# Twelve dense quads in layer 1's down projection, ten in layer 2's, and five-row products in the last norm

## The chip, the cores and the metric

The kernel runs on one core of a Trainium2 chip. The metric is the device time of one execution in microseconds; the median of three runs is compared. The core's engines work side by side and meet at semaphores: TensorE (PE; its weight loads are listed as PEld), VectorE (DVE), ScalarE (ACT), GpSimd (POOL) and SyncE (SP). In this kernel SP issues nearly all transfers, GpSimd a few.

## The reference

Two decoder layers over 256 tokens of width 2048, in float32. Layer 1 attends within one causal block (its list of past blocks is empty at this length), layer 2 in a sliding window of 128 with sinks. Each layer ends in a gated feed-forward with a causal convolution, and every sublayer is followed by a residual and a layer norm:

```
for layer in range(2):
    attn = moba(h) if layer == 0 else swa(h)
    h = layer_norm(ALPHA * h + attn, ln_g[layer, 0], ln_b[layer, 0])
    g, v = split(conv(h @ w_up) + conv_b)            # w_up: 2048 x 11008
    ffn  = (gelu(g) * v) @ w_down                    # w_down: 5504 x 2048
    h = layer_norm(ALPHA * h + ffn, ln_g[layer, 1], ln_b[layer, 1])
# layer_norm(x) = (x - mean) * rsqrt(var + eps) * g + b
```

## The kernel before

**Blocks and halves.** All matrix products run in the rounded format fp32r, three times each: every operand is split into a high and a low part, and high x high, high x low and low x high are added in PSUM. Weights come from DRAM in *halves*, tiles of 128 x 1024 numbers (0.5 MB), each of two *blocks* of 128 x 512. For each half SP loads `raw`, ScalarE rounds the high part `wh` (line 164), and VectorE subtracts to get the low part `wl` (line 173). Seven `raw` buffers and four pairs of `wh` and `wl` are in rotation, so a half is split when the half four before it has been used up. In a projection a block product is three matmuls of 512 columns: lines 389 to 391, or 618 to 620 where quads are used.

**Slots.** One step of the program order is one half. `take()` hands out the next half after it has emitted the split of the half three ahead; `at(n, f)` puts a small piece of work n halves later into the order. Every engine executes its own part of this order strictly in sequence.

**Quads.** In the down projection (43 k-blocks, four column chunks of 512, two token halves) a *quad* is 2 k-blocks x 2 column chunks x 2 token halves. A scheme of Strassen's kind makes it in 7 block products instead of 8. It needs sums of weight blocks, which are added up beforehand in DRAM (`sum_weights`: two copies on SP, three accumulating transfers on GpSimd, lines 301 to 309; `plan_sums` spreads them over earlier stages), and sums of activations (`pair_sums` and `four_sums`; for k-blocks 0 to 15 during the up projection, for later ones, the *late sums*, at the start of the down projection on VectorE and ScalarE). `QUADS[l][n]` is the number of quads of layer l for chunk pair n (0: chunks 0 and 1; 1: chunks 2 and 3; 2: the attention's output projection). `quad_halves` lays out the order: a few plain halves, then for each quad two halves of weight sums (`"t"`) and halves with single weight blocks, filled up with plain blocks, then the plain rest. The fourth single block of a quad shares a half with a plain block, or, where `DENSE` is true, with the fourth block of the next quad. In `two_chunks` the partial results `a`, `s1`, `s2`, `s3` are combined afterwards (`chain`) and added to the residual in `res`.

**Where late sums and scales live.** Two tiles `gb0` and `gb1` hold the norm's scale and shift, each loaded in four pieces (`load_gb_piece`). Before that they hold the early sums, and `gb1` also holds the late sums.

**The last norm.** The last eight halves of the last layer are multiplied token half by token half (`tilewise`, `late`), so that the first token half is normalised while the second is still being multiplied. For the second, `finish` computes, for three of the four chunks, `res * g * rs + (-mean * rs) * g + b`: the product `res * g` is made ahead (`scaled`), ScalarE scales it by `rs`, and TensorE makes the rest as a product of a 2-row matrix (`-mean * rs` and ones, transposed) with two rows `g` and `b` (line 692, in float32). VectorE adds the two and SP stores. The fourth chunk takes the plain way through `norm`.

Of the kernel before, what the change touches and what calls it, by code (L numbers as in the profile page):

```python
# [11 lines left out]
F32 = mybir.dt.float32  # L12
F32R = mybir.dt.float32r
# [39 lines left out]

QUADS = ((10, 8, 4), (10, 8, 4))
DENSE = ((False, True), (False, False))
LEAD = (4, 2)
# [3 lines left out]
S_EARLY = 8  # L60
QUAD_ORDER = ((0, 1, 2, 3, 4, 5, 8, 9, 6, 7), (0, 1, 2, 3, 4, 5, 6, 7))
QUAD_LIST = [(l, n, p) for l in range(2) for n in range(3) for p in range(QUADS[l][n])]
# [3 lines left out]
def quad_halves(l, n):  # L66

    if n == 2:  # L70
        return wo_halves(l)
    q = QUADS[l][n]
    plain = [(k, c) for c in range(2) for k in range(2 * q, FT)]
    two = lambda *b: ("w", *b, *(plain.pop(0) for _ in range(2 - len(b))))
    order = [two() for _ in range(LEAD[n])]
    fourth = []
    for p in QUAD_ORDER[n][:q]:
# [29 lines left out]
def trunk(ctx: ExitStack, tc: tile.TileContext, wst, wq, xT_in, x_in, relb, onehot, umask, sinks, conv_in, ln_g, ln_b, out):  # L107
# [363 lines left out]
    def project_out(src, nk, li, homes, preload, turnover=None, paired=None, early_sums=None, wo_sums=None):  # L471
# [45 lines left out]
        if not after:  # L517
            mr = stat.tile([P, 2], F32, name="mr", bufs=1)

# [25 lines left out]
        def quad_sums(p):  # L545
# [3 lines left out]
            if p < S_EARLY:  # L549
                return xT[:, 2 * p, :], xT[:, 2 * p + 1, :]  # L550
            o = (p - S_EARLY) * 1024
            return late_sums[:, o:o + 512], late_sums[:, o + 512:o + 1024]

        def two_chunks(n, which, scratch, at_half={}):
# [55 lines left out]
            for hx, ps in enumerate(steps):  # L610
# [12 lines left out]
                if ready and hx == max(first_end, quads_end):  # L623
# [3 lines left out]
                    for t in range(2):  # L627
                        at(4, measure, n, t)
                if not ready and hx == quads_end:
# [16 lines left out]
        def norm(t, c):  # L646
# [4 lines left out]
            if not after:  # L651
                nc.sync.dma_start(out[t * P:(t + 1) * P, cs], z)

        def rows():

            for i, a in enumerate((ln_g, ln_b)):
                nc.gpsimd.dma_start(paired[i:i + 1], bass.AP(tensor=a.tensor, offset=a.offset + li * D,
                                                             ap=[[D, 1], [1, (NCH - 1) * 512]]))
            nc.vector.memset(mr, 1.0)

# [4 lines left out]
        def last_piece(i):  # L665
# [7 lines left out]
            nc.vector.bn_stats(stats[:, 1, NCH - 1 + i, :], z[:, i * 256:(i + 1) * 256])  # L673

        def finish():


            nc.vector.tensor_scalar(mr[:, 0:1], ag[1][:, 0:1], rs[1], -1.0, op0=ALU.mult, op1=ALU.mult)
            mrT = wpool.tile([P, HW], F32, name="raw")[0:2, 0:P]
# [4 lines left out]
            nc.tensor.transpose(pt[0:2, 0:P], mr, ident)  # L684
            part = lambda n: res[:, 1, n * 512:(n + 1) * 512]
            by_rs = lambda n: nc.scalar.activation(part(n), part(n), AF.Copy, scale=rs[1])
            by_rs(0)
            nc.scalar.activation(mrT, pt[0:2, 0:P], AF.Copy)
            shift = []
            for n in range(NCH - 1):  # L690
                shift.append(psum.tile([P, 512], F32, name="at"))
                nc.tensor.matmul(shift[n], mrT, paired[0:2, n * 512:(n + 1) * 512], start=True, stop=True)
            norm(1, COLS[1][-1])
            for n in range(NCH - 1):
# [22 lines left out]
        def late(t, i):  # L717
            last = i == WINDOW - 1
            if t == 0 and last:
                evac(NCH - 1, 0, accs[0])  # L720
# [15 lines left out]
            if t == 1 and last:  # L736
                if after:
                    evac(NCH - 1, 1, accs[1])
                else:
                    last_piece(1)  # L740
                sd = moments(1)
                nc.vector.reciprocal(rs[1], sd)
                if not after:
                    finish()

        if paired is not None:
            late_sums = gbp.tile([P, D], F32R, name="gb1")
            gb = scale_shift()
            last_late = max(i for i, h in enumerate(quad_halves(l, 0)) if h[0] == "w" and h[1][0] // 2 in
                            range(S_EARLY, QUADS[l][0]))  # L750
# [108 lines left out]
    def layer_attention(l, rest, stage, turnover):  # L859
# [120 lines left out]
    class FeedForward:  # L980
# [26 lines left out]
        def run(self, rest):  # L1007
# [213 lines left out]
```

## Time and profile before

| What | us |
|---|---|
| Median of three runs (lowest to highest) | 2057.65 (2057.54 to 2058.45) |
| The profiled execution's own time | 2057.03 |
| Its span, first to last instruction | 2055.3 |
| Mean granted TensorE clock | 0.999 |
| First matmul with weights starts | 5.25 |
| Layer 1's down projection: quad stages, last window | 868 to 1068, to 1115 |
| Layer 2's down projection: quad stages, last window | 1823 to 2023, to 2045 |
| Last block product starts | 2044.65 |
| Last addition ends | 2051.41 |

A row of the timeline or of the chain reads: start in us, length in us, engine, line, operation, tile written and tiles read, shape, count; in brackets the engine's idle time ahead of it and what ended it. A row of waits reads: total us, number, longest. Instructions of a group that follow each other directly are merged into one row. A row of windows gives the stretch, its length, then busy us and instructions of each engine, the granted clock, the DMA engines' busy share and GB/s.

### The profile page before, as it was taken

How to read it: one execution, taken by the hardware profiler on the slowest of the kernel's cores; microseconds unless marked ns; L12 is line 12 of the kernel's file. 1: busy time of each engine (PE TensorE's matmuls, PEld its weight loads, DVE VectorE, ACT ScalarE, POOL GpSimd, SP SyncE). 2: the span in 40 equal slices, each digit the busy share in tenths (PEclk: the TensorE clock that was granted, in tenths of full speed). 3: DMA queues.
4: the chain of work that ended last, by engine and by line, in shares of the span. 5: the costliest groups of instructions: out<-in, count | busy, mean ns of one | idle time of the engine just before them, and what ended most of it. 6: DMA issues, size and time to landing. Idle time of an engine off the chain costs nothing.

```text
span 2055.3 us, 29510 instructions
## 1 busy us (share of the span) xinstructions
PE 2048.0 (100%) x10975; PEld 1770.4 (86%) x10975; DVE 1588.5 (77%) x2384; ACT 1073.4 (52%) x1494; POOL 131.4 (6%) x152
## 2 busy tenths in 40 slices
PE   9999999999999999999999999999999999999998
PEld 7888888988888888888888888898888888888887
DVE  5665558898887878787786787988887787887767
ACT  5554446345555455565563566545455554556553
POOL 0000000001111111000000100001111110000000
PEclk9999999999999999999999999999999999999999
DMA  9888768489999999689894967839999997568883
GB/s 321 252 267 268 225 193 302 178 248 301 286 296 308 280 306 240 211 280 311 294 333 130 259 191 222 328 123 296 291 283 292 287 289 238 189 211 314 286 298 125
DMA packets 166673, 532.04 MB, mean 259 GB/s; under 512 B 19152, under 2 KB 24080, under 8 KB 166272
## 3 DMA queue, kind: packets, MB, share of 16 engines
q1 hardware_dynamic: 138656, 479.11, 65.8%
q0 software_dynamic: 27584, 50.78, 16.1%
q8 instruction: 86, 1.41, 0.3%
q14 instruction: 59, 0.48, 0.1%
q10 hardware_dynamic: 288, 0.26, 0.0%
HBM read 527.91 MB, written 98.62 MB: 305 GB/s over the span
## 4 chain that ended last, share of the span: by engine, by line
PE 100%; DVE 0%; ACT 0%; issue 0%; POOL 0%; DVEq 0%; POOLq 0%
PE acc L336 39%; PE acc L339 20%; PE acc L620 6%; PE acc L618 6%; PE acc L619 6%; PE acc L389 4%; PE acc L391 4%; PE acc L390 4%; PE at L620 2%; PE at L619 2%; PE at L618 2%; PE acc L354 1%; PE acc L366 1%; PE at L809 1%; PE at L842 1%; PE at L707 1%
## 5 line engine op out<-in xcount | busy, mean ns | idle before, releaser
L173 DVE TENSOR_TENSOR wl<-raw,wh 128x1024 fp32r<-128x1024 f32 (+1 forms) x729 | 886.2, 1218 | 397.6 <-ACT wh L164 380.6
L164 ACT ACTIVATE wh<-raw 128x1024 fp32r<-128x1024 f32 (+1 forms) x729 | 769.3, 1056 | 709.3 <-issue 243.5
L336 PE MATMUL acc<-xT,wh 128*128 128x512 f32 x3456 | 872.7, 394 | 0.0
L336 PEld LDWEIGHTS acc<-xT,wh 128*128 128x128 f32 x3456 | 623.5, 189 | 113.0
L339 PEld LDWEIGHTS acc<-xT,wl 128*128 128x128 f32 x3456 | 471.5, 190 | 33.8
L339 PE MATMUL acc<-xT,wl 128*128 128x256 f32 x3456 | 481.9, 282 | 0.0
L618 PE MATMUL acc<-wh,up 128*128 128x512 f32 x328 | 127.6, 389 | 0.0
L619 PE MATMUL acc<-wl,up 128*128 128x512 f32 x328 | 127.6, 389 | 0.0
L620 PE MATMUL acc<-wh,up 128*128 128x512 f32 x328 | 127.6, 389 | 0.0
L1031 DVE SCALAR_TENSOR_TENSOR work<-work,cw 128x255 f32<-128x255 f32 x172 | 83.2, 484 | 6.1
L1032 DVE SCALAR_TENSOR_TENSOR work<-work,cw 128x254 f32<-128x254 f32 x172 | 83.1, 483 | 6.2
L305 POOL DMA_DIRECT2D t<-in_wq_dram x44 | 54.1, 1230 | 433.2 <-DMA t<-in_wq_dram 433.0
L1030 DVE TENSOR_SCALAR work<-work,cw 128x256 f32<-128x256 f32 x172 | 71.9, 418 | 6.2
L1029 DVE TENSOR_TENSOR work<-acc,work 128x256 f32<-128x256 f32 x172 | 71.7, 417 | 1.5 <-ACT work L1028 1.5
L620 PEld LDWEIGHTS acc<-wh,up 128*128 128x128 f32 x328 | 61.6, 188 | 12.7
L618 PEld LDWEIGHTS acc<-wh,up 128*128 128x128 f32 x328 | 61.6, 188 | 12.7
L619 PEld LDWEIGHTS acc<-wl,up 128*128 128x128 f32 x328 | 61.6, 188 | 12.7
L307 POOL DMA_DIRECT2D t<-t x44 | 36.5, 829 | 480.6 <-DMA t<-in_wq_dram 468.2
L1028 ACT ACTIVATE work<-acc 128x256 f32<-128x256 f32 x172 | 63.3, 368 | 6.5 <-PE acc L366 6.5
L201 ACT ACTIVATE work<-work 128x256 f32<-128x256 f32 x86 | 36.1, 419 | 48.1 <-DVE work L1032 48.1
L389 PE MATMUL acc<-wh,xT 128*128 128x512 f32 x144 | 57.9, 402 | 0.0
L391 PE MATMUL acc<-wh,xT 128*128 128x512 f32 x144 | 56.2, 390 | 0.0
(255 smaller groups left out, 2205.1 us busy)
## 6 DMA issues: line engine op xcount, KB each, us to landing
raw<-in_wst_dram SPq DMA_DIRECT2D x699, 512.0 KB, 5.5
t<-in_wq_dram SPq DMA_DIRECT2D x88, 512.0 KB, 7.3
raw<-t SPq DMA_DIRECT2D x88, 512.0 KB, 4.5
t<-in_wq_dram POOLq DMA_DIRECT2D x44, 512.0 KB, 11.6
t<-t POOLq DMA_DIRECT2D x88, 256.0 KB, 7.1
gb<-in_ln_g_dram SPq DMA_DIRECT2D x16, 256.0 KB, 6.5
gb<-in_ln_b_dram SPq DMA_DIRECT2D x16, 256.0 KB, 8.1
band<-ud SPq DMA_DIRECT2D x4, 512.0 KB
```

Source lines behind the costliest of these rows:

```text
L164: nc.scalar.activation(wh[:, c], raws[s][:, c], AF.Copy)
L173: nc.vector.tensor_tensor(out=wl[:, c], in0=raws[s][:, c], in1=wh[:, c].bitcast(F32), op=ALU.subtract)
L336: nc.tensor.matmul(acc, cols(wh, j), xT[:, k, :], start=(k == 0), stop=False)
L339: nc.tensor.matmul(o, cols(wl, j), xT[:, k, 0:T], start=False, stop=(k == KB - 1))
L389: nc.tensor.matmul(acc, sh, wh, start=(k == first), stop=False)
L390: nc.tensor.matmul(acc, sh, wl, start=False, stop=False)
L391: nc.tensor.matmul(acc, sl, wh, start=False, stop=(k == self.nk - 1))
L618: nc.tensor.matmul(bank(key), a[0], wh[:, c], start=key not in begun, stop=False)
L619: nc.tensor.matmul(bank(key), a[0], wl[:, c], start=False, stop=False)
L620: nc.tensor.matmul(bank(key), a[1], wh[:, c], start=False, stop=stop)
L1031: nc.vector.scalar_tensor_tensor(c[:, 1:T], h[:, 0:T - 1], w[:, 1:2], c[:, 1:T], op0=ALU.mult, op1=ALU.add)
L1032: nc.vector.scalar_tensor_tensor(c[:, 2:T], h[:, 0:T - 2], w[:, 0:1], c[:, 2:T], op0=ALU.mult, op1=ALU.add)
```

## The change

Layer 1's chunks 0 and 1 get twelve quads instead of ten, in the dense layout; layer 2's chunks 2 and 3 get ten instead of eight, dense as well, and take quads 8 and 9 first. Layer 1 then has four late sums, two of them in `gb0`, so that the scale's pieces are loaded later. The preparation of weight sums is spread anew over the stages. In the last norm the products have five rows instead of two and run in fp32r: `-g` in a high, a low and again a high part, `b` in a high and a low part, against the high and low part of `mean * rs` and ones. The rows are prepared ahead in `row_parts`, stored in DRAM and read back as rows. The fourth chunk's subtraction and scaling is cut in two 256-wide pieces, one of them ahead of the reciprocal (`centre`). The measuring of chunk 2's statistics in the last layer moves into the last eight halves.

```
-QUADS = ((10, 8, 4), (10, 8, 4))
-DENSE = ((False, True), (False, False))
+QUADS = ((12, 8, 4), (10, 10, 4))
+DENSE = ((True, True), (False, True))
...
-QUAD_ORDER = ((0, 1, 2, 3, 4, 5, 8, 9, 6, 7), (0, 1, 2, 3, 4, 5, 6, 7))
+QUAD_ORDER = ((0, 1, 2, 3, 4, 5, 8, 9, 10, 11, 6, 7), (8, 9, 0, 1, 2, 3, 4, 5, 6, 7))
+SUMS_AHEAD = (3, 2)
...
-            mr = stat.tile([P, 2], F32, name="mr", bufs=1)
+            mr = stat.tile([P, 5], F32R, name="mr", bufs=1)
+            parts = stat.tile([P, 5, 12], F32R, name="parts", bufs=1)
+            as_rows = dram.tile([5, (NCH - 1) * 512], F32, name="rows")
+            rank = []
...
-            o = (p - S_EARLY) * 1024
-            return late_sums[:, o:o + 512], late_sums[:, o + 512:o + 1024]
+            s, o = late_sums[(p - S_EARLY) // 2], p % 2 * 1024
+            return s[:, o:o + 512], s[:, o + 512:o + 1024]
...
-                        at(4, measure, n, t)
+                        if after or not n:
+                            at(4, measure, n, t)
...
+        def row_parts():
+            sg = stat.tile([P, 2, 12], F32, name="sg", bufs=1)
+            for i, a in enumerate((ln_g, ln_b)):
+                nc.gpsimd.dma_start(sg[:, i, :], bass.AP(tensor=a.tensor, offset=a.offset + li * D,
+                                                         ap=[[12, P], [1, 12]]))
+            nc.vector.tensor_scalar(sg[:, 0, :], sg[:, 0, :], -1.0, None, op0=ALU.mult)
+            for i in (0, 2):
+                nc.scalar.activation(parts[:, i, :], sg[:, 0, :], AF.Copy)
+            nc.scalar.activation(parts[:, 3, :], sg[:, 1, :], AF.Copy)
+            minus(parts[:, 1, :], sg[:, 0, :], parts[:, 0, :].bitcast(F32))
+            minus(parts[:, 4, :], sg[:, 1, :], parts[:, 3, :].bitcast(F32))
+            nc.gpsimd.dma_start(as_rows.rearrange("r (p c) -> p r c", c=12), parts.bitcast(F32))
+            nc.vector.memset(mr.bitcast(F32), 1.0)
+
         def rows():
...
-            nc.vector.memset(mr, 1.0)
+            nc.gpsimd.dma_start(paired[0:5, 0:(NCH - 1) * 512], as_rows)
+            for c, w in ((0, 1024), (1024, 512)):
+                rank.append(wpool.tile([P, HW], F32R, name="raw")[0:5, 0:w])
+                nc.scalar.activation(rank[-1], paired[0:5, c:c + w], AF.Copy)
...
+        def centre(half):
+            z = slice(D - 512 + half * 256, D - 256 + half * 256)
+            nc.vector.scalar_tensor_tensor(res[:, 1, z], res[:, 1, z], ag[1][:, 0:1], gb[0][:, z],
+                                           op0=ALU.subtract, op1=ALU.mult)
...
-            nc.vector.tensor_scalar(mr[:, 0:1], ag[1][:, 0:1], rs[1], -1.0, op0=ALU.mult, op1=ALU.mult)
+            mean = ag[1][:, 0:1]
+            nc.vector.tensor_scalar(mr[:, 0:1], mean, rs[1], None, op0=ALU.mult)
+            nc.vector.tensor_scalar(mr[:, 1:2], mean, rs[1], None, op0=ALU.mult)
+            nc.vector.scalar_tensor_tensor(mr[:, 2:3], mean, rs[1], mr[:, 0:1].bitcast(F32), op0=ALU.mult,
+                                           op1=ALU.subtract)
...
-                nc.tensor.matmul(shift[n], mrT, paired[0:2, n * 512:(n + 1) * 512], start=True, stop=True)
-            norm(1, COLS[1][-1])
+                nc.tensor.matmul(shift[n], mrT, rank[n // 2][:, n % 2 * 512:n % 2 * 512 + 512], start=True, stop=True)
+            centre(1)
+            z = slice(D - 512, D)
+            nc.vector.scalar_tensor_tensor(res[:, 1, z], res[:, 1, z], rs[1], gb[1][:, z], op0=ALU.mult, op1=ALU.add)
+            nc.sync.dma_start(out[P:2 * P, z], res[:, 1, z])
...
+            if t == 0 and not after and i == WINDOW // 2:
+                for s in range(2):
+                    measure(NCH - 2, s)
...
+                if not after:
+                    centre(0)
                 nc.vector.reciprocal(rs[1], sd)
...
-            late_sums = gbp.tile([P, D], F32R, name="gb1")
+            late_sums = [gbp.tile([P, D], F32R, name=f"gb{1 - i}") for i in range((QUADS[l][0] - S_EARLY) // 2)]
...
+            if len(late_sums) > 1:
+                first, late_gaps = last_of(S_EARLY + 2) + 5, (7, 11, 13, 15)
+            else:
+                first, late_gaps = 10, (8, 15, 22, 29)
             for n in range(NCH):
-                at(10 + 8 * n, load_gb_piece, n, 0)
-                at(last_late + (7, 11, 13, 15)[n], load_gb_piece, n, 1)
+                at(first + 8 * n, load_gb_piece, n, 0)
+                at(last_late + late_gaps[n], load_gb_piece, n, 1)
...
+            if not after:
+                at(40, row_parts)
...
-        plan_sums(WO_QUADS[l][2 * l:] + [(l, 0, p) for p in range(2)], (18, 2)[l], (12, 10)[l])
+        plan_sums(WO_QUADS[l] + [(l, 0, p) for p in range(SUMS_AHEAD[l])], (18, 2)[l], (11, 7)[l])
...
-            mine = [q for q in QUAD_LIST if q[0] == l and q[1] < 2][2:]
+            mine = [q for q in QUAD_LIST if q[0] == l and q[1] < 2][SUMS_AHEAD[l]:]
...
-                mine += WO_QUADS[1][:2]
...
-            plan_sums(mine, 12, (4 * FT - 30) / (len(mine) + 3))
+            plan_sums(mine, 0, (4 * FT - 18) / (len(mine) + 3))
```

More of the change, by code (lines that the diff above doesn't have):

```diff
@@ L76, in quad_halves @@
     fourth = []
-    for p in QUAD_ORDER[n][:q]:
+    for p in (p for p in QUAD_ORDER[n] if p < q):
         order += [("t", p, 0), two((2 * p, 0)), ("t", p, 1), two((2 * p + 1, 0))]
@@ L673, in last_piece @@
             nc.vector.bn_stats(stats[:, 1, NCH - 1 + i, :], z[:, i * 256:(i + 1) * 256])
+        def centre(half):
+            z = slice(D - 512 + half * 256, D - 256 + half * 256)
+            nc.vector.scalar_tensor_tensor(res[:, 1, z], res[:, 1, z], ag[1][:, 0:1], gb[0][:, z],
+                                           op0=ALU.subtract, op1=ALU.mult)
         def finish():
-            nc.vector.tensor_scalar(mr[:, 0:1], ag[1][:, 0:1], rs[1], -1.0, op0=ALU.mult, op1=ALU.mult)
-            mrT = wpool.tile([P, HW], F32, name="raw")[0:2, 0:P]
+            mean = ag[1][:, 0:1]
[3 more added lines that the diff above has]
+                                           op1=ALU.subtract)
+            mrT = wpool.tile([P, HW], F32R, name="raw")[0:5, 0:P]
             still = acc_tile()
@@ L683, in finish @@
             pt = psum.tile([P, 512], F32, name="at")
-            nc.tensor.transpose(pt[0:2, 0:P], mr, ident)
+            nc.tensor.transpose(pt[0:5, 0:P], mr.bitcast(F32), ident)
             part = lambda n: res[:, 1, n * 512:(n + 1) * 512]
@@ L687, in finish @@
             by_rs(0)
-            nc.scalar.activation(mrT, pt[0:2, 0:P], AF.Copy)
+            nc.scalar.activation(mrT, pt[0:5, 0:P], AF.Copy)
             shift = []
@@ L746, in project_out @@
         if paired is not None:
-            late_sums = gbp.tile([P, D], F32R, name="gb1")
+            late_sums = [gbp.tile([P, D], F32R, name=f"gb{1 - i}") for i in range((QUADS[l][0] - S_EARLY) // 2)]
             gb = scale_shift()
-            last_late = max(i for i, h in enumerate(quad_halves(l, 0)) if h[0] == "w" and h[1][0] // 2 in
-                            range(S_EARLY, QUADS[l][0]))
+            both = quad_halves(l, 0) + quad_halves(l, 1)
+            last_of = lambda p0: max(i for i, h in enumerate(both) if h[0] == "w" and
+                                     any(p0 <= k // 2 < QUADS[l][i >= len(quad_halves(l, 0))] for k, _ in h[1:]))
+            last_late = last_of(S_EARLY)
+            if len(late_sums) > 1:
+                first, late_gaps = last_of(S_EARLY + 2) + 5, (7, 11, 13, 15)
+            else:
+                first, late_gaps = 10, (8, 15, 22, 29)
             for n in range(NCH):
-                at(10 + 8 * n, load_gb_piece, n, 0)
-                at(last_late + (7, 11, 13, 15)[n], load_gb_piece, n, 1)
+                at(first + 8 * n, load_gb_piece, n, 0)
+                at(last_late + late_gaps[n], load_gb_piece, n, 1)
             for i, p in enumerate(range(0, S_EARLY, 2)):
```

3 lines of the change are left out of this document (removed).

## The prediction

> **What bounds the kernel now.** First the page, then who TensorE waits for:
>
> ```profile
> PE 2048.0 (100%) x10975; PEld 1770.4 (86%) x10975; DVE 1588.5 (77%) x2384; ACT 1073.4 (52%) x1494; POOL 131.4 (6%) x152
> ...
> PE at L264 <- POOL ident masks.py:199: 1.4, 1, 1.4
> PE at L684 <- DVE mr L678: 0.8, 1, 0.8
> PE at L692 <- ACT raw L688: 0.4, 1, 0.4
> ```
>
> The three waits lie before the first weight block and behind the last one. In between TensorE never waits, though a busy PE alone would not prove that, since its ends are modelled. So I went to the timeline for the distance between starts. These two rows are the first products of two blocks, thirteen blocks apart, each block three 512-wide products (L389, L390, L391):
>
> ```profile
> 2024.90 0.39 PE L389 MATMUL acc<-xT,up 128*128 128x512 f32 x1
> 2033.74 0.39 PE L389 MATMUL acc<-xT,up 128*128 128x512 f32 x1
> ```
>
> 8.84 us over 13 blocks is 0.680 us a block, 0.227 us a matmul. The 0.39 us is the length of one, not its price. What removes a block product removes 0.68 us, as long as weights arrive, and the tail behind the last product counts in full. Those are the two places where this change can earn; everywhere else it can only lose.
>
> **Block products.** A plain pair of k-blocks costs 8 block products for 2 token halves and 2 column chunks, a quad costs 7. Counting through the order of halves (`quad_halves`): layer 1, chunks 0 and 1, had 10 quads, 162 products in 58 halves; with 12 it has 160 in 61. Layer 2, chunks 2 and 3, had 8 quads, 164 products in 55 halves; with 10 it has 162 in 58. The other two stages keep theirs. Four products fewer: 4 x 0.680 = 2.72 us. This term rests on the start distance alone.
>
> The Trainium skill, "TensorE: Matmul & The Clock Gate", section "Back-to-back issue gap", gives about 131 ns per 512-wide matmul for a stream of load-and-multiply pairs; by that figure the term would be an estimated 12 x 0.131 = 1.6 us. Here the stream runs at 227 ns, so the measurement decides.
>
> **Do the weights keep up?** "Dense" packs two fourth blocks of two quads into one half, so fewer plain blocks lie between. In layer 1, chunks 0 and 1, the quad stretch goes from 130 products in 50 halves to 132 in 54: from 1.77 to 1.66 us of TensorE a half. A half is 0.524 MB, so it asks for 315 GB/s. Layer 1's second stage is already dense (88 products in 36 halves, the same 1.66 us). The three stretches are: the quad start of stage one, the middle of dense stage two, its end:
>
> ```profile
> 868.00:924.00 56.00, 56.00 (x250) 46.44 (x249) 46.23 (x53) 36.10 (x38) 0.00 (x0) 1.00 0.81 273
> 1005.00:1040.00 35.00, 35.00 (x156) 29.01 (x155) 25.62 (x21) 22.08 (x21) 0.00 (x0) 1.00 0.90 316
> 1040.00:1068.00 28.00, 28.00 (x126) 23.18 (x125) 27.68 (x30) 20.93 (x23) 0.00 (x0) 1.00 0.94 334
> ...
> ACT wh L164 <- PE acc L620: 35.8, 42, 1.7
> ```
>
> The columns after the engines' busy times are the clock, the DMA share and GB/s. Dense stage two moves 316 GB/s at a DMA share of 0.90, and 334 in the next stretch, with TensorE undisturbed. The last row (waits between 868 and 979 us) says that ScalarE's splits wait for TensorE to free a buffer, not for a load. So three more halves a stage cost nothing, covered by DMA room and by prefetch.
>
> A page's rule speaks against such density: the Trainium skill, "DMA: Bandwidth & Descriptors", section "Specifications", puts a core's share of HBM at about 358 GB/s. An estimate of 315 against 358 leaves 12% of room, so the rule, too, would allow the dense stream; the 334 GB/s measured here leaves 6%.
>
> VectorE is closer. Two more late sums (p = 10, 11) join layer 1's start, now four in a row, one every four halves. One late sum as the trace has it, with the splits between its pieces, and one split's lead:
>
> ```profile
> 892.74 1.23 DVE L173 TENSOR_TENSOR wl<-raw,wh 128x1024 fp32r<-128x1024 f32 x1 [0.46 <-ACT wh L164]
> 893.88 0.75 DVE L457 TENSOR_TENSOR work<-up 128x256 f32<-128x256 f32 x2
> 894.55 1.22 DVE L173 TENSOR_TENSOR wl<-raw,wh 128x1024 fp32r<-128x1024 f32 x1
> 895.69 0.81 DVE L440 TENSOR_TENSOR work<-work 128x128 f32<-128x128 f32 x3
> 896.42 0.28 DVE L449 TENSOR_TENSOR work<-work 128x128 f32<-128x128 f32 x1
> 896.62 1.22 DVE L173 TENSOR_TENSOR wl<-raw,wh 128x1024 fp32r<-128x1024 f32 x1
> 897.76 0.68 DVE L440 TENSOR_TENSOR gb<-work,gb 128x512 fp32r<-128x512 f32 x1
> 898.36 2.41 DVE L173 TENSOR_TENSOR wl<-raw,wh 128x1024 fp32r<-128x1024 f32 x2
> ...
> 900.49 1.06 ACT L164 ACTIVATE wh<-raw 128x1024 fp32r<-128x1024 f32 x1 [0.97 <-PE acc L620]
> 901.58 2.54 DVE L173 TENSOR_TENSOR wl<-raw,wh 128x1024 fp32r<-128x1024 f32 x2 [0.81 <-ACT wh L164]
> ```
>
> A sum takes 0.67 + 0.93 + 0.60 = 2.20 us from start to start, a split 1.14. Over the sixteen halves of four sums VectorE has 16 x 1.14 + 4 x 2.20 = 27.0 us of work, and one idle moment like the 0.46 us per two sums or so makes about 28; TensorE takes 16 x 1.66 = 26.6. The margin it eats: a split starts when the half four before it is used up, ends 1.09 + 1.22 = 2.31 us later, and is needed three halves (7 or 8 products, 4.8 to 5.4 us) after; about 2.2 us with the release. So some 1.5 of 2.2 us go, 0.5 to 1 is left: no stall, but the tightest place of the change. If the cover is gone it costs what is missing, at most the two new sums, 4.4 us. Behind it the margin refills by 1.66 - 1.14 us a half.
>
> **Sums in DRAM.** The quads' weight sums run on GpSimd's queue one after another, some 20.6 us each:
>
> ```profile
> 452.93 1.37 POOL L305 DMA_DIRECT2D t<-in_wq_dram  x1
> 473.51 1.35 POOL L305 DMA_DIRECT2D t<-in_wq_dram  x1
> ...
> 1719.12 0.81 POOL L309 DMA_DIRECT2D t<-t  x1 [6.43 <-DMA t<-t]
> 1115.00:1250.00 135.00, 135.00 (x794) 119.78 (x794) 101.05 (x230) 74.26 (x160) 12.43 (x14) 1.00 0.80 232
> ```
>
> Layer 2's attention goes from four to six of them (one every 7 halves), its feed-forward from 16 to 18, layer 1's from 18 to 17. Six need 124 us in a stretch of 135 at a DMA share of 0.80; the output projection's own four come first, from about 1140 us, and are done near 1225, before that projection begins at 1250. Layer 2's 18 need 371 us; they begin at half 0 instead of 12 (some 30 us earlier) and have two more to do (41 us), so they end some 11 us after the 1719 above; the projection that uses them begins at 1823 and loads its first about ten halves ahead. SP's loads would queue behind a sum that is late; none is. Zero. Moving layer 1's scale and shift pieces to halves 53 to 77 puts 0.26 MB transfers on SP where 4-product halves relax it; zero too.
>
> **The row parts.** At half 40 of layer 2's second stage four small VectorE and three small ScalarE instructions enter, and three transfers on GpSimd. Bounded by the 2x128 copy below (0.27 us), ScalarE's three are 0.8 us, and before them it waits one VectorE split, 1.2 us; the next split is 1.7 us late against a margin of 2.2. Zero, at worst 0.7. Their source transfer has nothing to wait for on GpSimd after 1719, so it lands long before. The two copies to the 5-row operand (at most 1.06 + 0.7 us) and the moved measurements (2 x 0.69) fall into idle time of 10.24 and 5.29 us, the first and second bracket here:
>
> ```profile
> 2046.22 0.29 ACT L640 ACTIVATE sd<-ag,eps 128x1 f32<-128x1 f32 x1 [10.24 <-DVE ag L638]
> 2033.94 0.69 DVE L514 TENSOR_TENSOR res<-acc,res 128x512 f32<-128x512 f32 x1 [5.29 <-PE acc L391]
> ```
>
> **The tail.** In order of time, and the width that `centre` uses:
>
> ```profile
> 2045.89 0.29 DVE L638 BATCH_NORM_AGGREGATE ag<-stats 128x2 f32<-128x30 f32 x1
> 2046.55 0.16 DVE L742 RECIPROCAL rs<-sd 128x1 f32<-128x1 f32 x1 [0.36 <-ACT sd L640]
> 2046.75 0.21 DVE L678 TENSOR_SCALAR mr<-ag,rs 128x1 f32<-128x1 f32 x1
> 2046.88 0.74 DVE L649 SCALAR_TENSOR_TENSOR res<-res,ag,gb 128x512 f32<-128x512 f32 x1
> 2047.01 0.27 PE L684 MATMUL at<-ident,mr 128*2 128x128 f32 x1 [0.77 <-DVE mr L678]
> 2047.38 0.27 ACT L688 ACTIVATE raw<-at 2x128 f32<-2x128 f32 x1
> 2047.56 1.32 ACT L686 ACTIVATE res<-res,rs 128x512 f32<-128x512 f32 x2
> 2047.65 0.75 DVE L650 SCALAR_TENSOR_TENSOR res<-res,rs,gb 128x512 f32<-128x512 f32 x1
> 2047.70 2.84 PE L692 MATMUL at<-work,raw 2*128 2x512 f32 x6 [0.42 <-ACT raw L688]
> 2048.86 0.69 DVE L514 TENSOR_TENSOR res<-at,res 128x512 f32<-128x512 f32 x1 [0.45 <-PE at L692]
> 2049.79 0.69 DVE L514 TENSOR_TENSOR res<-at,res 128x512 f32<-128x512 f32 x1 [0.24 <-PE at L692]
> 2050.65 0.76 DVE L514 TENSOR_TENSOR res<-at,res 128x256 f32<-128x256 f32 x2 [0.17 <-PE at L692]
> ...
> L1031 DVE SCALAR_TENSOR_TENSOR work<-work,cw 128x255 f32<-128x255 f32 x172 | 83.2, 484 | 6.1
> ```
>
> Now the three shift products pace VectorE: waits of 0.45, 0.24 and 0.17 us. In fp32r a 512-wide product starts every 0.227 us, if five rows go as fast as 128 do, instead of 0.95 us (2.84 / 3). Step by step: `centre(0)`, 0.48 us, fills the 0.36 us wait for the square root, so the reciprocal is 0.06 late. Three small instructions instead of one at 0.13 us (2046.75 to 2046.88) add 0.26: transpose at 2047.32, copy 2047.69, products 2048.01, the first ready at about 2048.5. VectorE meanwhile: `centre(1)` 2047.20, the second half of the norm 2047.71, first addition 2048.55, then 0.62, 0.62 and 0.34 on: end at 2050.55 instead of 2051.41. ScalarE's scalings move by 0.3 and stay ahead. The last output is issued and lands as long after the last addition as before, since five issues still find SP free. I take 0.8 us. From above: all waits and one 256-wide pass gone, 0.86 + 0.5 - 0.3 = 1.1. From below: five-row products no faster than those of two rows leave the 0.31 us delay, a loss of 0.3.
>
> **Sum.** 2.72 + 0.8 = 3.5 us, bounds 2.4 and 3.8. The profiled execution took 2057.03 us (span 2055.3), 0.6 below the median of 2057.65; its profile after should read about 2053.5, and the median 2057.65 - 3.5 = 2054.1, 0.17% faster. A difference of 0.2%, 4.1 us, is about what a measurement of this kernel can tell from no change, and the forecast falls just short of it.
>
> **Rivals.** *More than forecast* (0.14): even the upper bound, 3.8 us, lacks 0.3 us to 4.1; the three runs before spread over 0.9, so a median near 2053.3 can come out. *The late sums stall TensorE* (0.14): the 0.5 to 1 us of margin rests on durations read off one sum. Without it, 1 to 4.4 us come back: 2055.2 to 2058.5, mostly 2056. For it speaks VectorE at 46.23 of 56 us in that stretch before the change; against it, no wait there today. *Slower* (0.06): VectorE, in order, reaches the row parts and their source transfer has not landed; every weight split queues behind it, and TensorE behind those. The slowest kind of GpSimd's transfers:
>
> ```profile
> t<-in_wq_dram POOLq DMA_DIRECT2D x44, 512.0 KB, 11.6
> ```
>
> The last column is the median from issue to landing. If the row parts' source were issued only where it is used and took as long, 11.6 - 2.2 = 9.4 us would be lost: 2063.5. It decides once the landing is over 2.2 us late and cancels the gain at 5.7. Against it: GpSimd is free from about 1730 us, and that transfer is far smaller. That the change does not drop the four products would show as 10,975 minus less than twelve matmuls; I count it within the stall's chance, as its time is the same.
>
> **Numbers.** Forecast 0.66, with its own range of 2053.4 to 2055.2. The range 2053.2 to 2056.6 leaves out half of the first rival's lower part, the worst stalls and the slow rival, under 2 in 10. Faster 0.14, within 0.2% 0.80, slower 0.06.
>
> **What would show it.** TensorE's last product 2.7 us earlier; no new TensorE wait between 20 us and the tail, and VectorE busy over 90% around 880 to 910 us; three products in the tail within 0.9 us, and no idle of VectorE in front of the last additions; a wait of VectorE near 1999 us below 0.5 us. The forecast is wrong if the starts of the products near 905 us are more than 0.68 us a block apart, or if the tail is not shorter.

## The result and the profile after

| | before | after |
|---|---|---|
| Median us (17 runs each) | 2057.86 (2057.33 to 2058.70) | 2054.07 (2053.47 to 2054.37) |
| Profiled execution us, span | 2057.03, 2055.3 | 2054.26, 2052.5 |

The ratio is 0.9981, with a 95% interval of 0.9975 to 0.9988: 3.8 us less, where 3.5 was forecast. By the bound of 0.2% this is no difference; by its interval it is a small gain.

The page after, its engines' row, and what TensorE waited for:

```profile
PE 2043.9 (100%) x10960; PEld 1767.8 (86%) x10960; DVE 1600.8 (78%) x2410; ACT 1081.4 (53%) x1507; POOL 143.7 (7%) x166
...
PE at L265 <- POOL ident masks.py:199: 1.4, 1, 1.4
PE at L714 <- DVE mr L707: 1.1, 1, 1.1
PE at L722 <- ACT raw L718: 0.4, 1, 0.4
```

Fifteen matmuls fewer: four products of three, and three in the tail, where six float32 instructions became three. No new wait stands between the start and the tail. Where the time went shows in the timeline of TensorE, as the first product of each quad stage and the first product behind it. After:

```profile
868.86 0.40 PE L622 MATMUL acc<-wh,up 128*128 128x512 f32 x1
1067.45 0.39 PE L390 MATMUL acc<-xT,up 128*128 128x512 f32 x1
...
1822.19 0.40 PE L622 MATMUL acc<-wh,up 128*128 128x512 f32 x1
2020.77 0.39 PE L390 MATMUL acc<-xT,up 128*128 128x512 f32 x1
```

and before:

```profile
868.25 0.40 PE L618 MATMUL acc<-wh,up 128*128 128x512 f32 x1
1068.20 0.39 PE L389 MATMUL acc<-xT,up 128*128 128x512 f32 x1
...
1822.91 0.40 PE L618 MATMUL acc<-wh,up 128*128 128x512 f32 x1
2022.86 0.39 PE L389 MATMUL acc<-xT,up 128*128 128x512 f32 x1
```

Layer 1's two stages took 199.95 us and take 198.59, layer 2's 199.95 and 198.58: 1.36 and 1.37 us, two products of 0.680 each. (The profiled execution after reaches its first quad stage at 868.86, 0.6 us later than the one before, so its last block product starts only 2.08 us sooner. This differs between executions: the ten other profiles with the same first stage reach it between 868.02 and 868.80.)

The tight place, VectorE's four late sums. The windows are before and after from 880 to 910 us (busy us per engine, clock, DMA share, GB/s), each of its own kernel:

```profile
880.00:910.00 30.00, 30.00 (x134) 24.82 (x134) 25.78 (x33) 20.08 (x21) 0.00 (x0) 1.00 0.88 293
```

```profile
880.00:910.00 30.00, 30.00 (x134) 24.86 (x133) 29.27 (x45) 21.30 (x22) 0.00 (x0) 1.00 0.84 278
```

The timeline after has, behind that stretch, four splits and the first two products of the half that the first of them serves:

```profile
912.03 4.95 DVE L174 TENSOR_TENSOR wl<-raw,wh 128x1024 fp32r<-128x1024 f32 x4
914.45 0.39 PE L622 MATMUL acc<-wh,st 128*128 128x512 f32 x1
914.67 0.39 PE L623 MATMUL acc<-wl,st 128*128 128x512 f32 x1
```

VectorE went from 86 to 98% busy, and the split that ends at 913.25 (912.03 and one split of 1.22) leads the first product of its half by 1.20 us, and the second, which is the one that reads `wl`, by 1.42. That is the smallest lead of the four sums. Counted in the same way before, to the first product, no lead was under 1.9.

The row parts, on GpSimd, VectorE and ScalarE:

```profile
1727.74 0.88 POOL L665 DMA_DIRECT2D sg<-in_ln_g_dram  x1
...
2003.49 0.17 DVE L667 TENSOR_SCALAR sg<-sg 128x12 f32<-128x12 f32 x1
2003.69 0.31 ACT L669 ACTIVATE parts<-sg 128x12 fp32r<-128x12 f32 x2 [1.38 <-DVE sg L667]
2005.15 3.50 DVE L174 TENSOR_TENSOR wl<-raw,wh 128x1024 fp32r<-128x1024 f32 x3 [0.83 <-ACT wh L165]
```

GpSimd fetched their source 276 us ahead of its use. ScalarE waited 1.38 us for VectorE's split, as reckoned. The smallest lead of a split behind it is 1.47 us; before, the smallest there was 2.24.

The tail, in order of time:

```profile
2044.13 0.48 DVE L698 SCALAR_TENSOR_TENSOR res<-res,ag,gb 128x256 f32<-128x256 f32 x1
2044.54 0.15 DVE L780 RECIPROCAL rs<-sd 128x1 f32<-128x1 f32 x1
2044.98 0.22 DVE L707 SCALAR_TENSOR_TENSOR mr<-ag,rs,mr 128x1 fp32r<-128x1 f32 x1
2045.25 0.27 PE L714 MATMUL at<-ident,mr 128*5 128x128 f32 x1 [1.09 <-DVE mr L707]
2045.62 0.27 ACT L718 ACTIVATE raw<-at 5x128 fp32r<-5x128 f32 x1 [0.17 <-PE at L714]
2045.63 0.75 DVE L725 SCALAR_TENSOR_TENSOR res<-res,rs,gb 128x512 f32<-128x512 f32 x1
2045.94 0.96 PE L722 MATMUL at<-raw 5*128 5x512 f32 x3 [0.42 <-ACT raw L718]
2046.47 1.95 DVE L515 TENSOR_TENSOR res<-at,res 128x512 f32<-128x512 f32 x4
2047.19 1.94 SPq L733 DMA_DIRECT2D out_dram<-res  x4
```

Three products in 0.96 us instead of 2.84, and the four additions in one row without an idle moment. From the start of the last block product (of its last matmul, to be exact: 2042.57; before 2044.65) to the end of the last addition it is 5.86 us instead of 6.75. So far the forecast holds to 0.1 us. But the last output packet ends 8.44 us after that product instead of 8.63, and the last store lands, that is, signals its completion, 9.02 us after it instead of 9.35: of the 0.9 us only 0.2 to 0.3 is left. The DMA rows show where the rest stayed (windows of 1 us; the last two columns are the DMA engines' busy share and GB/s). After:

```profile
2046.40:2047.40 1.00, 0.50 (x3) 0.06 (x1) 0.93 (x2) 0.71 (x2) 0.00 (x0) 1.00 0.14 55
2047.40:2048.40 1.00, 0.00 (x0) 0.00 (x0) 1.00 (x3) 0.00 (x0) 0.00 (x0) 0.86 0.93 346
2048.40:2049.40 1.00, 0.00 (x0) 0.00 (x0) 0.02 (x1) 0.00 (x0) 0.00 (x0) 0.50 1.04 339
2049.40:2050.40 1.00, 0.00 (x0) 0.00 (x0) 0.00 (x0) 0.00 (x0) 0.00 (x0) 0.50 0.94 285
```

and before:

```profile
2049.40:2050.40 1.00, 1.00 (x3) 0.18 (x1) 0.76 (x2) 0.00 (x0) 0.00 (x0) 1.00 0.56 217
2050.40:2051.40 1.00, 0.14 (x1) 0.00 (x0) 0.83 (x3) 0.00 (x0) 0.00 (x0) 0.56 0.71 279
2051.40:2052.40 1.00, 0.00 (x0) 0.00 (x0) 0.00 (x1) 0.00 (x0) 0.00 (x0) 0.50 0.99 357
2052.40:2053.40 1.00, 0.00 (x0) 0.00 (x0) 0.00 (x0) 0.00 (x0) 0.00 (x0) 0.50 0.53 151
```

Before, the stores came far enough apart to leave the DMA engines gaps. After, they are full for three microseconds, two of them behind the last addition.

One more step follows the landing. SyncE closes the program with a row of waits, one for each transfer's semaphore, in a fixed order and some 0.06 us apart. What it waited for there, before and after:

```profile
SPq L1216 <- DMA out_dram<-res: 1.8, 1, 1.8
```

```profile
SPq L1261 <- DMA out_dram<-res: 1.8, 3, 0.9
```

Before, the last two stores signal semaphores that stand near the head of this row, so SyncE waits once, for 1.8 us, and then still steps through six more: 1.27 us from the last landing to the span's end. After, the last store signals the last of the row, and 0.90 us are left. So the span ends 9.92 us after the last block product instead of 10.61, 0.69 sooner: 0.33 from the earlier landing, and 0.37 from the place of a semaphore in a row, which has nothing to do with the additions. The prediction has no such term.

### The profile page after: what moved, and what is told of

Same layout as the page of the kernel before. It is cut to its first block, busy times and chain, and to the rows that moved or that the text cites. A ratio compares the mean times of both kernels' runs of the same rounds, so it can differ in the third digit from the quotient of the medians.

```text
span 2052.5 us, 29568 instructions
## 1 busy us (share of the span) xinstructions
PE 2043.9 (100%) x10960; PEld 1767.8 (86%) x10960; DVE 1600.8 (78%) x2410; ACT 1081.4 (53%) x1507; POOL 143.7 (7%) x166
## 4 chain that ended last, share of the span: by engine, by line
PE 99%; DMA 0%; DVE 0%; ACT 0%; issue 0%; DVEq 0%; ACTq 0%
PE acc L337 39%; PE acc L340 20%; PE acc L623 6%; PE acc L624 6%; PE acc L622 6%; PE acc L390 4%; PE acc L392 4%; PE acc L391 4%; PE at L623 2%; PE at L624 2%; PE at L622 2%; PE acc L355 1%; PE acc L367 1%; PE at L855 1%; PE at L888 1%; PE at L740 1%
## 5 line engine op out<-in xcount | busy, mean ns | idle before, releaser
L622 PE MATMUL acc<-wh,up 128*128 128x512 f32 x304 | 118.3, 389 | 0.0
L623 PE MATMUL acc<-wl,up 128*128 128x512 f32 x304 | 118.3, 389 | 0.0
L624 PE MATMUL acc<-wh,up 128*128 128x512 f32 x304 | 118.3, 389 | 0.0
L306 POOL DMA_DIRECT2D t<-in_wq_dram x48 | 58.9, 1226 | 321.1 <-DMA t<-in_wq_dram 320.8
L308 POOL DMA_DIRECT2D t<-t x48 | 39.6, 826 | 545.3 <-DMA t<-in_wq_dram 545.3
L622 PEld LDWEIGHTS acc<-wh,up 128*128 128x128 f32 x304 | 57.1, 188 | 11.9
L623 PEld LDWEIGHTS acc<-wl,up 128*128 128x128 f32 x304 | 57.1, 188 | 11.8
L624 PEld LDWEIGHTS acc<-wh,up 128*128 128x128 f32 x304 | 57.1, 188 | 11.7
L310 POOL DMA_DIRECT2D t<-t x48 | 39.2, 816 | 334.1 <-DMA t<-t 327.3
L390 PE MATMUL acc<-wh,xT 128*128 128x512 f32 x144 | 57.8, 402 | 0.1
```

What stands on the lines that cost most here:

```text
L390: nc.tensor.matmul(acc, sh, wh, start=(k == first), stop=False)
L622: nc.tensor.matmul(bank(key), a[0], wh[:, c], start=key not in begun, stop=False)
L623: nc.tensor.matmul(bank(key), a[0], wl[:, c], start=False, stop=False)
L624: nc.tensor.matmul(bank(key), a[1], wh[:, c], start=False, stop=stop)
```

## The experiments

Eleven kernels were run; unless a text says otherwise each is the changed kernel with one edit. Differences are medians of 11 runs against the kernel before on the same chip.

**The quads alone.**

```
-            mr = stat.tile([P, 5], F32R, name="mr", bufs=1)
+            mr = stat.tile([P, 2], F32, name="mr", bufs=1)
...
-            mrT = wpool.tile([P, HW], F32R, name="raw")[0:5, 0:P]
+            mrT = wpool.tile([P, HW], F32, name="raw")[0:2, 0:P]
...
-            centre(1)
...
+            norm(1, COLS[1][-1])
```

> The quads and their schedule as changed, the last norm as before. Theory (block products and tail add up): four products of 0.680 us fewer, so 2.7 us under the kernel before; the down projections' quad stages shorter by 1.36 us each in the profile, and from the last block product to the last addition 6.8 us as before. Rival (the tail gives nothing, and the other 1.1 us of the 3.8 measured come from the new schedule of the weight sums): 3.8 us under the kernel before, with some stage other than the two quad stages shorter.

Measured: 2054.22 against 2057.44, 3.2 us less (ratio 0.9985, 0.9976 to 0.9993). From first to last block product the profile has 2036.66 us instead of 2039.40, 2.74 less; the quad stages take 198.63 and 198.59 us, the others what they took before, and the last addition comes 6.75 us after the last product, as before. The rival falls in the profile: no other stage is shorter. The time's 3.2 against 2.7 is within its interval; besides, the last store lands 9.35 us after the last product, as before, but signals the last semaphore of SyncE's row, and the span ends 0.90 us behind the landing instead of 1.27.

**The tail alone.**

```
-QUADS = ((12, 8, 4), (10, 10, 4))
-DENSE = ((True, True), (False, True))
+QUADS = ((10, 8, 4), (10, 8, 4))
+DENSE = ((False, True), (False, False))
```

> The quads as before (ten and eight in each layer, layouts as before), the last norm and the order of weight sums as changed. Theory: 0.8 us (0.3 to 1.1) under the kernel before, all of it behind the last block product, where the last addition comes 0.9 us sooner; no stage of TensorE shorter. Rival (the output's transfers end the run, not the additions, so an earlier addition gains nothing): no difference, with the last landing as long after the last block product as before, about 9.2 us.

Measured: 2057.04 against 2057.44, 0.4 us less (0.9997, 0.9988 to 1.0006, so not to be told from nothing by the times). In the profile the last addition comes 5.86 us after the last product, 0.9 sooner, the last packet 8.53, 0.1 sooner, and the last landing 9.01, 0.34 sooner; SyncE's closing waits take 1.27 us, as before. The theory's 0.9 is right for VectorE, and its 0.8 for the time, which the interval alone would allow, is about twice what the landing gained; the rival is nearer.

**Twelve quads in layer 2's first stage too.**

```
-QUADS = ((12, 8, 4), (10, 10, 4))
-DENSE = ((True, True), (False, True))
+QUADS = ((12, 8, 4), (12, 10, 4))
+DENSE = ((True, True), (True, True))
```

> Layer 2's chunks 0 and 1 with twelve dense quads as well; all else as changed. Theory (a block product is worth its 0.680 us wherever the weights keep up): 1.36 us under the changed kernel, 5.1 under the kernel before, with layer 2's quad stages at 197.2 us. The smallest lead of a weight split at the four late sums of layer 2 near 1.2 us, as in layer 1. Rival (VectorE's late sums in layer 2 meet the shift and scale loads, or GpSimd's 20 weight sums come late): TensorE waits near 1850 us or behind a sum, and the gain is gone.

Measured: 2052.76 against 2057.44, 4.7 us less (0.9978, 0.9969 to 0.9987). Its layer 2 stages, in the timeline:

```profile
1821.53 0.40 PE L622 MATMUL acc<-wh,up 128*128 128x512 f32 x1
2018.80 0.39 PE L390 MATMUL acc<-xT,up 128*128 128x512 f32 x1
```

and VectorE at the late sums there, in a window:

```profile
1833.00:1863.00 30.00, 30.00 (x134) 24.86 (x133) 29.28 (x47) 20.98 (x22) 0.00 (x0) 1.00 0.87 284
```

197.27 us, 1.32 less than the changed kernel, with VectorE at 98% and TensorE never waiting. The smallest lead of a split there is again 1.20 us. The same block product is worth the same there in the profile; by the times it is 0.9 to 1.1 us less than the two medians of the changed kernel, on other chips. This kernel had the lowest median of all that were run.

**Late sums made heavier.**

```
             for p in range(S_EARLY, QUADS[l][0]):
+                if l == 0:
+                    at(S_EARLY // 2 + 3 + 4 * (p - S_EARLY), sums(p)[0])
+                    at(S_EARLY // 2 + 4 + 4 * (p - S_EARLY), sums(p)[1])
```

> The changed kernel, with the first two steps of each late sum in layer 1 done twice (1.6 us more of VectorE for each of four). Theory (VectorE's lead there is some 1.2 us and refills by about 0.5 us a half): TensorE waits about 5 us in all (4 to 6.4) between 895 and 920 us, none elsewhere. Rival (the lead is larger than read, or the scheduler of the engines hides it): under 2 us.

Measured: 2058.91 in one run, and layer 1's stages take 203.43 us, 4.84 more. The waits of TensorE, and the four of its rows that end one:

```profile
PE acc L623 <- DVE wl L174: 2.3, 2, 1.3
...
PE at L623 <- DVE wl L174: 0.9, 2, 0.7
```

```profile
900.22 0.50 PE L623 MATMUL acc<-wl,st 128*128 128x512 f32 x1 [1.06 <-DVE wl L174]
908.57 0.50 PE L623 MATMUL acc<-wl,st 128*128 128x512 f32 x1 [1.25 <-DVE wl L174]
913.92 0.50 PE L623 MATMUL at<-wl,st 128*128 128x512 f32 x1 [0.29 <-DVE wl L174]
916.92 0.50 PE L623 MATMUL at<-wl,xT 128*128 128x512 f32 x1 [0.66 <-DVE wl L174]
```

6.4 us of work added, 4.8 lost, in the place and within the bounds expected: the lead was real and no larger than read. The listed waits come to 3.2 us, since they count from a modelled end. Counted between starts, the four products above, a fifth at 918.66 and the product behind each of them come 4.7 us late in all, which is the whole loss.

**The row parts' source on SyncE's queue.**

```
-                nc.gpsimd.dma_start(sg[:, i, :], bass.AP(tensor=a.tensor, offset=a.offset + li * D,
+                nc.sync.dma_start(sg[:, i, :], bass.AP(tensor=a.tensor, offset=a.offset + li * D,
```

> The changed kernel with the two source transfers of the row parts issued on SyncE's queue instead of GpSimd's, so that they are issued where they are used and queue behind weight loads. Theory (the slow rival's mechanism exists and is spared only because GpSimd issues early): VectorE waits 3 to 6 us for them near 2003 us, TensorE 1 to 5 us, and the time is that much over the changed kernel's. Rival (VectorE's lead covers it): no TensorE wait.

Measured: 2061.63 in one run, some 8 us above the changed kernel; layer 2's stages take 205.53 us, 6.94 more. VectorE's wait and TensorE's, in the timeline:

```profile
2009.76 0.17 DVE L667 TENSOR_SCALAR sg<-sg 128x12 f32<-128x12 f32 x1 [6.25 <-DMA sg<-in_ln_g_dram]
...
2011.44 0.79 PE L622 MATMUL at<-wh,xT 128*128 128x512 f32 x1 [3.50 <-ACT wh L165]
```

and the window that holds them:

```profile
2010.00:2016.00 6.00, 4.09 (x9) 2.91 (x10) 4.93 (x7) 4.99 (x8) 0.94 (x1) 0.53 0.36 60
```

Two transfers of 6 KB held VectorE for 6.25 us, just over the 3 to 6 expected. TensorE waited 4.0 (3.5 and 0.5), inside the expected bounds, but lost 6.9: the granted clock of that window is 0.53, and one product took 0.79 us instead of 0.40. Counted between starts, the two products that waited lost 4.7 us, and those behind them, 0.427 us apart instead of 0.227, the other 2.2. The wait was followed by slow products, which the expectation did not have.

**The changed kernel again**, as measure for the next five (the early store, the last chunk's store left out and the two-row products ran on the same chip, the other two on another).

> The changed kernel once more, beside the next three on the same chip, as their measure. 3.8 us under the kernel before; last addition 5.86 us after the last block product starts, span's end 9.9 to 10.4 us after it.

Measured: 2053.94 against 2057.52, 3.6 us less; last addition 5.86, last packet 8.45 and span's end 9.92 us after the last product.

**The first half of the last chunk stored early, and one store left out.**

```
-            centre(1)
-            z = slice(D - 512, D)
-            nc.vector.scalar_tensor_tensor(res[:, 1, z], res[:, 1, z], rs[1], gb[1][:, z], op0=ALU.mult, op1=ALU.add)
-            nc.sync.dma_start(out[P:2 * P, z], res[:, 1, z])
+            for half in range(2):
+                if half:
+                    centre(1)
+                z = slice(D - 512 + half * 256, D - 256 + half * 256)
+                nc.vector.scalar_tensor_tensor(res[:, 1, z], res[:, 1, z], rs[1], gb[1][:, z], op0=ALU.mult, op1=ALU.add)
+                nc.sync.dma_start(out[P:2 * P, z], res[:, 1, z])
```

> The changed kernel, but the last chunk's first 256 columns are finished and stored before the second are centred: the first output of the tail is issued 0.8 us sooner, there is one more 256-wide VectorE step and one more issue. Theory A (the output's transfers, a megabyte on 16 full queues, end the run): the last packet and the span's end come 0.3 to 0.5 us sooner after the last block product than in the changed kernel. Theory B (the last addition and its own store's landing end the run): no sooner, or 0.1 to 0.2 us later for the added step.

and, in the other kernel, leaving the step as it was:

```
-            nc.sync.dma_start(out[P:2 * P, z], res[:, 1, z])
```

> The changed kernel without the store of the second token half's last chunk (a quarter of the tail's output is left out). Last addition and last issue as in the changed kernel. Theory A (transfers end the run): the last packet comes 0.4 to 0.7 us sooner. Theory B (the last addition ends it): no change beyond 0.1 us.

Measured: 3.4 us less than before in both (2054.15 and 2054.08 against 2057.52), last packet 8.47 and 8.46 us after the last product, the changed kernel's 8.44 and 8.45; last landing 9.07 and 9.10 against 9.02 and 9.00. Neither came sooner. As put, theory A fell: it counted the whole megabyte as one queue. In the changed kernel the first store's packets end about when the first addition's begin, so taking it away frees nothing that is waited for.

**Another store left out.**

```
-                    nc.sync.dma_start(out[P:2 * P, n * 512:(n + 1) * 512][:, c], z)
+                    if n:
+                        nc.sync.dma_start(out[P:2 * P, n * 512:(n + 1) * 512][:, c], z)
```

> The changed kernel without the store of the second token half's first chunk, whose store is the first of the three additions (a quarter of the tail's output is left out). The store left out before was done before the others queued up; this one stands at the head of the three. Theory A, mended (the transfers of the three added chunks, 768 KB on full queues, end the run): last packet 0.6 us (0.4 to 0.8) sooner after the last block product, time 0.3 to 0.7 us lower than the changed kernel's 3.6 to 3.8 us under the kernel before. Theory B (the last addition and its own landing end it): no change beyond 0.15 us.

Measured: 2053.61 against 2057.57, 4.0 us less, 0.2 to 0.4 beyond the changed kernel, which the times alone cannot tell from nothing; last packet 7.89 us after the last product, 0.55 sooner, and last landing 8.68, 0.34 sooner, with the last addition where it was:

```profile
2047.30:2048.30 1.00, 0.00 (x0) 0.00 (x0) 1.00 (x3) 0.00 (x0) 0.00 (x0) 1.00 0.58 219
2048.30:2049.30 1.00, 0.00 (x0) 0.00 (x0) 0.07 (x1) 0.00 (x0) 0.00 (x0) 0.63 0.72 269
2049.30:2050.30 1.00, 0.00 (x0) 0.00 (x0) 0.00 (x0) 0.00 (x0) 0.00 (x0) 0.50 0.85 255
```

The mended theory holds: the stores of the three added chunks, issued within 1.5 us, queue on the DMA engines and end the run.

**Two-row float32 products, centring kept.** The edit is that of the first experiment, but `centre` stays as changed.

> The changed kernel with the two-row float32 products of before, the centring in two pieces kept. Theory (the five-row products in fp32r are what shortens VectorE's chain, the transfers then take most of it back): last addition 6.4 to 6.6 us after the last block product instead of 5.86, the span's end 0.2 to 0.5 us later than the changed kernel's. Rival (the centring alone brings the tail's gain): last addition 6.2 or sooner, span's end within 0.1 us of the changed kernel's.

Measured: 2054.54 against 2057.52, 3.0 us less, 0.6 later than the changed kernel. The profiled execution was the longest of its eleven (2055.24) and missed the expected 6.4 to 6.6 us by far: 8.51. Its windows tell why:

```profile
2045.00:2046.00 1.00, 1.00 (x3) 0.51 (x4) 0.44 (x1) 1.00 (x2) 0.00 (x0) 1.00 0.00 0
2046.00:2050.00 4.00, 3.53 (x5) 0.91 (x3) 1.74 (x4) 0.17 (x1) 0.00 (x0) 0.50 0.46 180
```

and its products in the timeline:

```profile
2045.00 4.53 PE L715 MATMUL at<-work,raw 2*128 2x512 f32 x6 [0.42 <-ACT raw L711]
```

At 2046.00, 3.8 us after the last block product (it ended at 2042.16), the granted clock fell to half with the products still under way: 4.53 us for what took 2.84 at full clock. The theory's direction holds, the size of this one profile does not speak for the median.

**No centring.**

```
-            centre(1)
...
+            norm(1, COLS[1][-1])
...
-                if not after:
-                    centre(0)
```

> The changed kernel with the fourth chunk's norm in two 512-wide steps after the reciprocal, as before; the five-row products kept. Theory (the products set the last additions, and one 256-wide step ahead of the reciprocal saves little): the first output is issued 0.2 us later, the last addition comes 0 to 0.2 us later, the time stays within 0.3 us of the changed kernel's. Rival (the centring is what the tail's gain rests on): 0.4 us or more later.

Measured: 2054.06 against 2057.57, 3.5 us less; last addition 5.87 us and last packet 8.64 us after the last product. The first store comes 0.2 us later, runs into the next one's packets, and the last packet is 0.2 later; the time does not tell it from the changed kernel.

## Why the prediction was right, point by point

- **Block products (2.72 us).** Right: 2.73 in the two stages' profiles, 2.74 in the kernel with the quads alone, and 1.32 for two products fewer still. The price per product, read as the distance between starts and not as the 0.39 us of one, carried the sum. Fifteen fewer matmuls in the page fit the count.
- **Weights keep up.** Right. The dense start of layer 1 cost nothing. The margin of VectorE's splits was put at 0.5 to 1 us and is 1.20 to 1.42; the doubled sums lost 4.8 us where the margin ended, so the stall rival was a real mechanism, and the change stayed on the near side of it by that margin. (The room of 6% that the prediction gives for the stream works out at 7%.)
- **Sums in DRAM.** Right: GpSimd's last sum was issued at 1727.21, forecast about 1730; TensorE waits for none.
- **Row parts.** Right: zero, with 1.4 us of ScalarE's wait (1.2 reckoned) and 0.8 us taken from the lead of the splits (2.24 to 1.47; 1.7 reckoned). The slow rival's mechanism exists: issued where it is used, the same small transfer costs 6.9 us in the stage. The change is spared because GpSimd, with nothing else to do, issues it 276 us ahead.
- **Tail (0.8 us).** The mechanism on TensorE and VectorE was right (last addition 0.89 us sooner after the last product, 0.86 forecast), the step behind it failed: "the last output is issued and lands as long after the last addition as before, since five issues still find SP free". SP was free, the DMA engines were not. Additions 0.6 us apart send 256 KB stores 0.6 us apart, faster than the engines empty them: at the 339 to 346 GB/s of their full windows a store takes an estimated 0.76 to 0.77 us, so the stores queue. The last packet came 0.2 us sooner and the last landing 0.33, and by the times the tail is worth 0.4 (alone), or 0.4 to 0.6 (changed kernels of two measurements against the quads alone).
- **Sum.** 3.5 forecast, 3.8 measured, 3.6 (the changed kernel again) and 3.5 (without centring) in two further measurements of kernels with both parts. The 3.8 counts from a median before of 2057.86 over 17 runs; from the 2057.65 that the forecast started with it would be 3.6. By the traces the block products give 2.72, the earlier landing 0.33 and the place of the last semaphore in SyncE's row 0.37: 3.4 in all. Added up in the same way from their traces, the quads alone come to 3.1 (3.2 measured), the tail alone to 0.3 (0.4) and the kernel with twelve quads in layer 2 as well to 4.7 (4.7); for the other kernels measured in eleven runs it falls 0.2 to 0.4 short, the two-row float32 kernel left aside, whose profile has the slow products. What is left over is within the interval of each measurement (2.7 to 3.7 us wide) and is not assigned. That the sum came so close is luck in part: the tail's term was more than twice what the landing gained, and SyncE's closing waits, which the prediction left out, made up for most of it. That these waits are the cause is read from the traces; no run changes them alone. (The forecast's own range is also wider at its lower end, 2053.4, than its upper bound of 3.8 us gives, 2053.85.)

## What to carry to other kernels

Price a removed matmul by the distance between starts in its stream, and then look for the engine that feeds the stream: its lead over the consumer, in microseconds at the tightest place, says whether the gain arrives. A small transfer that an in-order engine waits for was free here on a queue that ran 276 us ahead; on the queue that paces itself by the work the same transfer held VectorE for 6.25 us. Where the end of a run is a burst of stores, as here, bringing the additions closer helps until the stores touch each other; behind that point the DMA engines, not the arithmetic, set the end. And before a few tenths of a microsecond are put down to a change, look at what the program does behind its last landing: here 0.90 to 1.33 us, by which semaphore the last store happens to signal.

## What the runs showed of the hardware that was not expected

**The clock falls inside the tail.** The granted clock went to 0.50 at 2046.00 in the kernel with two-row float32 products, in the midst of them, and at 2050.5 in the profile before, as its last product ended (2050.54). In the former, 2.84 us of products became 4.53. The changed kernel's three products ended at 2046.90, ahead of the fall at 2048.1. In the kernel without the last chunk's store the fall came in the midst of them, at 2045.7: they took 1.27 us instead of 0.96, and the last addition still came 5.86 us after the last block product. So short a group has little to lose. It fits that the runs of the kernel before spread over 1.9 us in the last two measurements (2057.03 to 2058.94) and those of the changed kernel over 1.1 (2053.42 to 2054.55; but 54 runs against 11, and with 17 runs each it is 1.4 against 0.9), and that the former's longer runs carry the lower mean clock; a part of the tail's worth may be that. No run was made to separate it.

Where the fall comes is not set by the kernel alone. In all thirteen profiles each stretch at full clock lasts a whole number of 3.413 us steps (2041.17 us is 598 of them, 2044.58 is 599), and the first stretch begins between 4.1 and 7.4 us after the first instruction, differently from execution to execution. The fall then comes anywhere between 3.6 and 6.5 us after the last block product ends: 3.8 in the two-row float32 kernel, 5.6 before, 5.3 after. That it hit the products in one profile and missed them in another is chance of the execution as far as these profiles go.

The Trainium skill, "TensorE: Matmul & The Clock Gate", section "What's actually happening", lets the clock halve after an idle window of about 3.4 us. The profiles agree with the length of the window, but not with the word idle: in the 3.41 us ahead of the fall TensorE was busy for 0.9 to 3.0 us (3.0 before, with its two-row products), and in the late-source kernel the clock fell 2.4 us into a wait.

**A stall is dearer than its wait.** The 4.0 us of TensorE's wait for the late source cost 6.9 us: the granted clock fell to 0.50 at 2010.39, within the wait, and stayed there until 2017.22, two of the 3.413 us steps, while the products that followed started 0.427 us apart instead of 0.227.
